# A hybrid S5, RWKV-7 and PEER decoder step on one core: dense pools opened with the last step, the sample's finish through a GpSimd transfer, finishing loads spread out, low-rank products of 64 rows, a last pick that is not held

## The chip, the cores and the metric

The kernel runs on one core of one Trainium2 chip. The metric is the device time of one execution in microseconds. It is written in Bass with the Tile framework.

## The reference, cut to what matters

One layer is run on a prompt (512 tokens) and on a sample group (8 x 8 = 64 tokens), d = 1024, float32. An adaLN-modulated RMSNorm feeds one input projection; its columns go to an S5 state-space mixer and to an RWKV-7 mixer of 8 heads. The low-rank part of RWKV that the change touches, and the PEER layer that takes most of the time:

```
w_raw = -softplus(-(w0 + tanh(w_lo) @ w2)) - 0.5      # w_lo: 64 columns
a = sigmoid(a0 + a_lo @ a2)                           # a_lo: 64 columns
...
q = (xb @ w_q).reshape(128, 8, 2, 64)                 # 8 retrieval heads
s1, s2 = q[:, :, 0] . keys1, q[:, :, 1] . keys2       # 128 keys each
v1, i1 = top_k(s1, 16); v2, i2 = top_k(s2, 16)
sc, pos = top_k(v1 + v2 over 16 x 16 pairs, 16)       # 16 of 16384 experts
idx = take(i1 * 128 + i2, pos); gate = softmax(sc)
act = gelu(einsum(u_tab[idx], xb))
ff = einsum(gate * act, v_tab[idx])
```

Then y = final RMSNorm(x + ga2 * ff), where x already holds the mixers' output.

## The kernel before, in words

Tokens are cut in tiles: tile 0 is the sample (64 tokens, held twice, so that each half of the partitions has four of the eight heads), tiles 1 to 4 are 128 prompt tokens each. They are taken in the order 1, 2, 3, 0, 4.

Phase 1 does the norm, the input projection and S5. Then five steps are woven: step i runs `back` (RWKV state) of a tile, `front` (RWKV's decay, keys and triangular inverse) of a later one, `select` (output projection, second norm, query and key scores), `pick` (the top 16s on VectorE) of the tile before, and `gbuild` of one of the tiles 1 to 3. `front` has the low-rank products (lines 923 to 928): W2 holds w2 in rows 0 to 63 of one half and a2 in rows 64 to 127 of the other, with zeros elsewhere; for each of the two halves four matmuls over 128 rows are followed by four activations.

Tiles 1, 2 and 3 (DENSE) go through all 16384 experts. `gbuild` writes their gates as a dense matrix: per 4 tokens (a step of its loop) two one-hot matrices B and A (tiles "ab") are made on ScalarE, VectorE or GpSimd, four matmuls multiply them, and ScalarE copies the result to Gst; per 16 tokens Gst goes to DRAM (Gd, line 1508). For the last of the three, the ab buffers are 15 in a pool of their own (gp2), and the 8 expert blocks of group 0 are copied from Gst into G0 (line 1505). `dense` then does 128 blocks of 128 experts: ur is 128 columns of u transposed; uh and ul are its rounded part and the rest; 24 matmuls give scores pd (line 1520); ScalarE applies gelu to wf (1605); VectorE multiplies the gates (1607); wf and the rows vr of v are split in the same way (1610 to 1623), and 18 matmuls add to the outputs po (1627), which stay in six PSUM banks. Blocks come in groups of 8 (GBL), each with its gates loaded from Gd (line 1525) at remainder 2 of the group before. The tokens' vectors hf are loaded, rounded and split to dh and dl once (1555, 1562, 1563).

Tiles 0 and 4 gather their experts' rows (`bulk`): 64 and 128 indirect loads of u rows on GpSimd's queue, a dot product on VectorE each (1449), gelu, then as many loads of v rows and accumulations (1459). Three gathers are issued per block. At the end of tile 0 two matmuls with a folding matrix add the two halves of acc (1465), ScalarE copies them to h2 (1466), and `finish` adds the residual, norms and stores. `finish` of the tiles 1 to 3 follows block 127. What `finish` needs is loaded by `open_finish`, one load per block from block 32 (FB).

The order of each engine's instructions is fixed when the program is built: Tile's scheduler models times and takes, per engine, what is ready in its model, the earlier line first. A pool that is opened takes memory that closed pools gave back, and its tiles wait for the tiles that were there. `issue_after(x)` keeps what is inside from being placed ahead of x. All loads and stores but the gathers and h2 are issued by SP.

Of the kernel before, what the change touches and what calls it, by code (L numbers as in the profile page):

```python
# [6 lines left out]
F32 = mybir.dt.float32  # L7
# [15 lines left out]
KB = 8  # L23
# [155 lines left out]
class Kernel:  # L179
# [6 lines left out]
    PB = {"r": 3, "s": 3, "h": 1, "g": 1}  # L186
    UX, UWT, AB2 = 0, 0.5, 15
    UG = True
    UO = -100000
    PO, GO, SO, RO, FO = {}, {}, {4: 4000}, {}, {}  # L190
    FB = 32
    PW = 3.0
# [10 lines left out]
    OHB = 2  # L203
    EU, ED = True, False
    UR = "s"
# [27 lines left out]
    def ps(self, shape, g="r"):  # L233
        t = (self.psA if g == "g" else self.psB).tile([128, 512], F32, name="pa" + g, bufs=self.PB[g])
        return shaped(t, shape[1:])[:shape[0]]
# [616 lines left out]
    def open_rwkv(self):  # L852
# [14 lines left out]
        SY.dma_start(rst, I["rst"])  # L867
        W2 = wp.tile([128, 2, 512], F32)
        g2 = wp.tile([128, 512], F32)
        G.memset(W2, 0.0)  # L870
        SY.dma_start(W2[0:64, 0, :], I["wa2"][0:64, :])
        SY.dma_start(W2[64:128, 1, :], I["wa2"][64:128, :])
        SY.dma_start(g2, I["g2"])
# [28 lines left out]
    def front(self, ti):  # L902
# [19 lines left out]
        sg = t4([8, W])  # L922
        for i in range(2):
            pz = ps([128, 4, W], "r")
            for j in range(4):
                T.matmul(pz[:, j, :], W2[:, i, j * 128:(j + 1) * 128], lt, start=True, stop=True)
            for j in range(4):
                S.activation(sg[:, 4 * i + j, :], pz[:, j, :], AF.Tanh, bias=hw0[:, 4 * i + j:4 * i + j + 1], scale=0.5)
# [504 lines left out]
    def bulk(self, ti, c0, nk, ei, gt):  # L1433
# [27 lines left out]
        if smp:  # L1461
            ffs = []
            for n in range(2):
                pf = self.ps([64, 512], "g")
                T.matmul(pf, self.fold, acc[:, n * 512:(n + 1) * 512], start=True, stop=True)
                S.copy(h2[:64, n * 512:(n + 1) * 512], pf)
            self.finish(0, [h2[:64]])
        else:
            self.finish(ti, [acc])

    def gbuild(self, d):
        V, S, G, T, SY = self.nc.vector, self.nc.scalar, self.nc.gpsimd, self.nc.tensor, self.nc.sync
        iob = self.iota[:, None, :].to_broadcast([128, 4, 128])
        n = self.TG
        gp, nb = (self.gp2, self.AB2) if d == 2 and self.AB2 else (self.gp, self.AB)
        for tg in range(128 // n):
            Gst = self.gs.tile([128, 128, n], F32, name="Gst")
            for q in range(n // 4):
                t0 = d * 128 + tg * n + q * 4

                def bc(t):
                    return t[:, t0:t0 + 4, None].to_broadcast([128, 4, 128])
                oh = gp.tile([128, 128, 4], BF16, name="oh", bufs=self.OHB)
                B = gp.tile([128, 4, 128], F32, name="ab", bufs=nb)
# [19 lines left out]
            if d == 2:  # L1504
                V.tensor_copy(self.G0[:, d * (128 // n) + tg], Gst[:, 0:self.GBL, :])
                if tg == 0:
                    self.loadG(self.G0, 0, d * (128 // n))
            SY.dma_start(self.Gd[d * (128 // n) + tg], Gst.rearrange("p n t -> p (n t)"))
# [19 lines left out]
    def open_dense(self):  # L1528
# [6 lines left out]
        if self.EU:  # L1535
            self.ue = sc.pool("ue", **kw)
        if self.ED:
            self.dp = sc.pool("dp", 1, **kw)
        self.G0 = sc.pool("g0", 1, **kw).tile([128, N // self.TG, self.GBL, self.TG], F32, name="G0")
        self.sh = Scope(self.tc)  # L1540
        self.hf = self.sh.pool("hf", **kw).tile([128, KB, N], F32, name="hf")
        if self.AB2:
# [10 lines left out]
        for d, ti in enumerate(self.DENSE):  # L1553
            sl = slice(128 * d, 128 * d + 128)
            SY.dma_start(self.hf[:, :, sl], self.h2d[ti].rearrange("p (k t) -> p k t", k=KB))

    def dense(self):
# [3 lines left out]
        N = 128 * nd  # L1561
        S.copy(self.dh, self.hf)
        V.tensor_tensor(self.dl, self.hf, self.dh.bitcast(F32), op=OP.subtract)
        self.sh.close()
# [3 lines left out]
        ue = self.ue if self.EU else sp.pool("ue", **kw)  # L1568
        up = sp.pool("up", 2, **kw)
        dp = self.dp if self.ED else sp.pool("dp", 1, **kw)  # L1570
        pso = sp.pool("pso", 1, space=PSUM, **kw)
# [7 lines left out]

        GO = dp.tile([128, N // TG, GBL, TG], F32, name="G1")  # L1580

# [12 lines left out]
        with self.tc.issue_after(self.kld.ins):  # L1594
            pa = first(0)
            G1 = self.G0
        for b in range(128):
            if b % GBL == 0:
                Gr = G1
            if b % GBL == self.GPF and b + GBL < 128:  # L1600
                with self.tc.issue_after(self.kld.ins):
                    G1 = (self.G0, GO)[(b // GBL + 1) % 2]
                    self.loadG(G1, b // GBL + 1)
# [26 lines left out]
        warm = self.sm.tile([128, 1], F32, name="ss")  # L1630
        S.activation(warm, self.iota[:, :1], AF.Sqrt)
        for d in range(nd):
            self.finish(self.DENSE[d], outs[2 * d:2 * d + 2], G if d in self.FP else V)

    def run(self, stop=None):
# [50 lines left out]
        else:  # L1686
            dense, gs = self.dense(), self.gathers()
            n = m = 0.0
            for b, r in enumerate(dense):
                m += self.PW  # L1690
                while m >= 1 and pk:
                    m -= 1
                    with tc.issue_after(self.gv.ins):
                        live = next(pk, 0)
                    if live == 0:
                        pk = None
                        self.sx.close()
                if b >= self.FB:
                    if b == self.FB:
                        fl = self.open_finish()  # L1700
                    with tc.issue_after(self.vld.ins):
                        next(fl, None)
# [40 lines left out]
```

## Time and profile before

| | us |
|---|---|
| median of 3 runs | 1920.74 (1916.82 to 1923.91) |
| the profiled execution: time / span | 1923.54 / 1921.8 |
| TensorE busy | 1771.2 (92%) |
| VectorE busy | 1512.5 (79%) |
| ScalarE busy | 803.6 (42%) |
| GpSimd busy | 676.7 (35%) |

The span is that of the profiled execution alone. A view by stretch gives the busy microseconds of each engine in it, TensorE's granted clock (1.00 is full speed), the busy share of the DMA engines and what they moved. In a timeline a bracket at the end of a row gives the idle time of the engine before it, and what ended it.

### The profile page before, as it was taken

How to read it: one execution, taken by the hardware profiler on the slowest of the kernel's cores; microseconds unless marked ns; L12 is line 12 of the kernel's file. 1: busy time of each engine (PE TensorE's matmuls, PEld its weight loads, DVE VectorE, ACT ScalarE, POOL GpSimd, SP SyncE). 2: the span in 40 equal slices, each digit the busy share in tenths (PEclk: the TensorE clock that was granted, in tenths of full speed). 3: DMA queues.
4: the chain of work that ended last, by engine and by line, in shares of the span. 5: the costliest groups of instructions: out<-in, count | busy, mean ns of one | idle time of the engine just before them, and what ended most of it. 6: DMA issues, size and time to landing. Idle time of an engine off the chain costs nothing.

```text
span 1921.8 us, 32723 instructions
## 1 busy us (share of the span) xinstructions
PE 1771.2 (92%) x12299; PEld 1531.6 (80%) x12299; DVE 1512.5 (79%) x3081; ACT 803.6 (42%) x1468; POOL 676.7 (35%) x540
## 2 busy tenths in 40 slices
PE   8899987988879797789999999999999999999994
PEld 5699645758558676779999998899999999999993
DVE  7958324495996968779988878798788878888898
ACT  4232515535764677733333333433333333333332
POOL 0000201000351334334544444364444445444554
PEclk9899998999889898989999999999999999999998
DMA  8524654544346586679999998899999999999995
GB/s 328 158 88 105 201 179 146 185 149 152 119 137 211 181 295 232 233 264 338 330 375 334 351 357 325 270 389 349 340 353 322 338 352 330 336 341 355 325 322 190
DMA packets 202206, 513.30 MB, mean 267 GB/s; under 512 B 26232, under 2 KB 87800, under 8 KB 197952
## 3 DMA queue, kind: packets, MB, share of 16 engines
q1 hardware_dynamic: 146464, 308.82, 47.1%
q0 software_dynamic: 55584, 202.40, 28.9%
q8 instruction: 96, 1.57, 0.3%
q14 instruction: 62, 0.51, 0.1%
HBM read 470.36 MB, written 39.62 MB: 265 GB/s over the span
## 4 chain that ended last, share of the span: by engine, by line
PE 52%; DVE 11%; issue 5%; POOL 4%; ACT 3%; DMA 2%; POOLq 0%; SPq 0%; ACTq 0%; DVEq 0%
PE pd L1520 24%; PE po L1627 23%; POOL gr L1444 3%; PE pas L1268 2%; DVE oh L1486 1%; DVE ab L1493 1%; DMA ur<-u_t 1%; DVE t2s L1306 1%; DVE idxu L1308 1%; DVE idxu L1305 1%; ACT ab L1490 1%; PE par L1501 0%; ACT Gst L1502 0%; PE pag L1501 0%; PE par L997 0%
## 5 line engine op out<-in xcount | busy, mean ns | idle before, releaser
L1444 POOL DMA_INDIRECT gr<-v_tab,ei x192 | 259.5, 1352 | 276.0 <-DVE acc L1459 246.4
L1520 PE MATMUL pd<-dh,uh 128*128 128x384 f32 x1024 | 346.3, 338 | 10.6 <-ACT wf L1605 10.6
L1520 PE MATMUL pd<-dh,ul 128*128 128x384 f32 x1024 | 345.7, 338 | 0.0
L1444 POOL DMA_INDIRECT gr<-u_tab,ei x192 | 247.3, 1288 | 278.4 <-DVE scr L1449 230.2
L1520 PE MATMUL pd<-dl,uh 128*128 128x384 f32 x1024 | 345.1, 337 | 0.0
L1516 ACT CAST uh<-ur 128x1024 fp32r<-128x1024 f32 x128 | 134.5, 1051 | 271.5 <-PE pd L1520 264.4
L1459 DVE SCALAR_TENSOR_TENSOR acc<-gr,act,acc 128x1024 f32<-128x1024 f32 x190 | 244.1, 1285 | 2.9 <-DMA gr<-v_tab,ei 1.5
L1627 PE MATMUL po<-vl,wh 128*128 128x512 f32 x768 | 237.8, 391 | 1.8 <-DVE vl L1623 1.8
L1627 PE MATMUL po<-vh,wl 128*128 128x512 f32 x768 | 236.7, 390 | 0.0
L1449 DVE SCALAR_TENSOR_TENSOR scr<-gr,h 128x1024 bf16<-128x1024 f32 x192 | 234.2, 1220 | 2.2 <-DMA gr<-u_tab,ei 1.3
L1517 DVE TENSOR_TENSOR ul<-ur,uh 128x1024 fp32r<-128x1024 f32 x128 | 157.3, 1229 | 71.5 <-ACT uh L1516 71.3
L1520 PEld LDWEIGHTS pd<-dh,uh 128*128 128x128 f32 x1024 | 194.0, 189 | 18.3 <-ACT wf L1605 12.4
L1627 PE MATMUL po<-vh,wh 128*128 128x512 f32 x768 | 200.3, 395 | 5.8 <-ACT vh L1622 5.8
L1520 PEld LDWEIGHTS pd<-dl,uh 128*128 128x128 f32 x1024 | 193.9, 189 | 4.9
L1610 ACT CAST wh<-wf 128x384 fp32r<-128x384 f32 x128 | 65.8, 514 | 311.8 <-PE po L1627 253.1
L1520 PEld LDWEIGHTS pd<-dh,ul 128*128 128x128 f32 x1024 | 193.7, 189 | 0.4
L1623 DVE TENSOR_TENSOR vl<-vr,vh 128x1024 fp32r<-128x1024 f32 x128 | 156.5, 1223 | 25.0 <-ACT vh L1622 24.8
L1627 PEld LDWEIGHTS po<-vl,wh 128*128 128x128 f32 x768 | 143.9, 188 | 33.8 <-DVE vl L1623 2.7
L1627 PEld LDWEIGHTS po<-vh,wl 128*128 128x128 f32 x768 | 144.2, 188 | 31.0
L1627 PEld LDWEIGHTS po<-vh,wh 128*128 128x128 f32 x768 | 141.2, 188 | 32.4 <-ACT vh L1622 9.3
L1622 ACT CAST vh<-vr 128x1024 fp32r<-128x1024 f32 x128 | 134.4, 1050 | 50.7 <-PE po L1627 38.2
L1498 POOL TENSOR_TENSOR ab<-oh,dix 128x512 f32<-128x512 bf16 x72 | 87.5, 1222 | 178.4 <-DVE oh L1486 64.2
(472 smaller groups left out, 2986.4 us busy)
## 6 DMA issues: line engine op xcount, KB each, us to landing
ur<-u_t SPq DMA_DIRECT2D x128, 512.0 KB
vr<-v_tab SPq DMA_DIRECT2D x128, 512.0 KB
Gd<-Gst SPq DMA_DIRECT2D x24, 1024.0 KB
G<-Gd SPq DMA_DIRECT2D x15, 1536.0 KB
wo<-w_out SPq DMA_DIRECT2D x40, 512.0 KB
wq<-w_q SPq DMA_DIRECT2D x40, 512.0 KB
wt<-w_ada SPq DMA_DIRECT2D x32, 512.0 KB
wr<-w_in SPq DMA_DIRECT2D x18, 512.0 KB
```

The lines of the kernel that those rows point to most:

```text
L1268: T.matmul(pt[:, hh, :], wq[:, k, :], hT[:, k, :], start=(k == 0), stop=(k == KB - 1))
L1444: G.indirect_dma_start(out=r, out_offset=None, in_=I[tab], in_offset=bass.IndirectOffsetOnAxis(ap=ei[:, k:k + 1], axis=0))
L1449: V.scalar_tensor_tensor(scr, r, 1.0, h2, op0=OP.mult, op1=OP.mult, accum_out=act[:, k:k + 1])
L1459: V.scalar_tensor_tensor(acc, r, act[:, k:k + 1], acc, op0=OP.mult, op1=OP.add)
L1498: G.tensor_tensor(A, oh, bc(self.dix[:, 1]), op=OP.mult)
L1516: nc.scalar.copy(uh, ur)
L1517: self.mark = nc.vector.tensor_tensor(ul, ur, uh.bitcast(F32), op=OP.subtract).ins
L1520: nc.tensor.matmul(pa, u[:, k, :], h[:, k, :], start=(k == 0 and i == 0), stop=(k == KB - 1 and i == 2))
L1610: S.copy(wh, wf)
L1622: S.copy(vh, vr)
L1623: V.tensor_tensor(vl, vr, vh.bitcast(F32), op=OP.subtract)
L1627: T.matmul(outs[2 * d + n], w[:, d * 128:(d + 1) * 128], v[:, n * 512:(n + 1) * 512], start=(b == 0 and i == 0), stop=(b == 127 and i == 2))
```

## The change

Pools `up` and `dp` are opened with the dense pools, before step 4, and both gate tiles lie there; hf becomes three parts that pass through the `ur` buffers. `gbuild` of the last tile copies the blocks of groups 0 and 1, and loads both groups' other tokens; it takes 4 ab buffers from gp2 for every third step and otherwise those of gp. The pick of tile 4 is not held behind the last gate instruction of VectorE. The finishing loads come one per 8 blocks from block 14. The sample's halves are added by a transfer and VectorE. Sqrt's table is asked for by an activation that reads the last wf.

```diff
-    UX, UWT, AB2 = 0, 0.5, 15
+    UX, UWT, AB2 = 0, 0.5, 4
-    FB = 32
+    FB = 14
-    EU, ED = True, False
+    EU, ED = True, True
@@ open_rwkv
-        W2 = wp.tile([128, 2, 512], F32)
+        W2 = wp.tile([128, 512], F32)
-        G.memset(W2, 0.0)
-        SY.dma_start(W2[0:64, 0, :], I["wa2"][0:64, :])
-        SY.dma_start(W2[64:128, 1, :], I["wa2"][64:128, :])
+        SY.dma_start(W2, I["wa2"])
@@ front
-        for i in range(2):
-            pz = ps([128, 4, W], "r")
-            for j in range(4):
-                T.matmul(pz[:, j, :], W2[:, i, j * 128:(j + 1) * 128], lt, start=True, stop=True)
+        pzs = [ps([128, 4, W], "r") for _ in range(2)]
+        for j in range(4):
+            for i in range(2):
+                sl = slice(64 * i, 64 * i + 64)
+                T.matmul(pzs[i][:, j, :], W2[sl, j * 128:(j + 1) * 128], lt[sl], start=True, stop=True)
+        for i, pz in enumerate(pzs):
@@ bulk
-            ffs = []
-            for n in range(2):
-                pf = self.ps([64, 512], "g")
-                T.matmul(pf, self.fold, acc[:, n * 512:(n + 1) * 512], start=True, stop=True)
-                S.copy(h2[:64, n * 512:(n + 1) * 512], pf)
+            G.dma_start(h2[:64], acc[64:128])
+            yield
+            V.tensor_tensor(h2[:64], h2[:64], acc[:64], op=OP.add)
             self.finish(0, [h2[:64]])
@@ gbuild
-        gp, nb = (self.gp2, self.AB2) if d == 2 and self.AB2 else (self.gp, self.AB)
+                gp, nb = (self.gp2, self.AB2) if d == 2 and (tg * n // 4 + q) % 3 == 2 else (self.gp, self.AB)
-                oh = gp.tile([128, 128, 4], BF16, name="oh", bufs=self.OHB)
+                oh = self.gp.tile([128, 128, 4], BF16, name="oh", bufs=self.OHB)
-                V.tensor_copy(self.G0[:, d * (128 // n) + tg], Gst[:, 0:self.GBL, :])
-                if tg == 0:
-                    self.loadG(self.G0, 0, d * (128 // n))
+                for g, t in enumerate(self.G2_):
+                    V.tensor_copy(t[:, d * (128 // n) + tg], Gst[:, g * self.GBL:(g + 1) * self.GBL, :])
+                    if tg == 0:
+                        self.loadG(t, g, d * (128 // n))
@@ open_dense
-        if self.ED:
-            self.dp = sc.pool("dp", 1, **kw)
-        self.G0 = sc.pool("g0", 1, **kw).tile([128, N // self.TG, self.GBL, self.TG], F32, name="G0")
+        self.up, self.dp = sc.pool("up", 2, **kw), sc.pool("dp", 1, **kw)
+        self.G2_ = [self.dp.tile([128, N // self.TG, self.GBL, self.TG], F32, name="G%d" % i) for i in range(2)]
-        self.hf = self.sh.pool("hf", **kw).tile([128, KB, N], F32, name="hf")
-            SY.dma_start(self.hf[:, :, sl], self.h2d[ti].rearrange("p (k t) -> p k t", k=KB))
+            hf = self.ud.tile([128, KB, 128], F32, name="ur", bufs=2)
+            SY.dma_start(hf, self.h2d[ti].rearrange("p (k t) -> p k t", k=KB))
+            S.copy(self.dh[:, :, sl], hf)
+            V.tensor_tensor(self.dl[:, :, sl], hf, self.dh.bitcast(F32)[:, :, sl], op=OP.subtract)
@@ dense
-        S.copy(self.dh, self.hf)
-        V.tensor_tensor(self.dl, self.hf, self.dh.bitcast(F32), op=OP.subtract)
-        up = sp.pool("up", 2, **kw)
-        dp = self.dp if self.ED else sp.pool("dp", 1, **kw)
+        up, dp = self.up, self.dp
-        GO = dp.tile([128, N // TG, GBL, TG], F32, name="G1")
-            G1 = self.G0
+            G1 = self.G2_[0]
             if b % GBL == self.GPF and b + GBL < 128:
-                with self.tc.issue_after(self.kld.ins):
-                    G1 = (self.G0, GO)[(b // GBL + 1) % 2]
+                G1 = self.G2_[(b // GBL + 1) % 2]
+                if b > GBL:
                     self.loadG(G1, b // GBL + 1)
-        S.activation(warm, self.iota[:, :1], AF.Sqrt)
+        S.activation(warm, wf[:, :1], AF.Sqrt, scale=0.0)
@@ run
-                    with tc.issue_after(self.gv.ins):
-                        live = next(pk, 0)
+                    live = next(pk, 0)
-                if b >= self.FB:
+                if b >= self.FB and b % 8 == self.FB % 8:
```

## Rows read from the trace of the kernel before

**Rows 1.** Stretches: start:end and length; busy us (x instructions) per engine; clock; DMA.
```profile
850.00:1886.00 1036.00, 1031.70 (x5197) 934.37 (x5197) 875.22 (x1092) 369.05 (x505) 495.56 (x375) 1.00 0.94 337
...
775.00:806.00 31.00, 24.67 (x206) 22.91 (x205) 26.04 (x93) 30.05 (x78) 15.58 (x12) 1.00 0.46 185
806.00:850.00 44.00, 33.53 (x146) 30.32 (x145) 36.04 (x173) 16.14 (x20) 10.44 (x10) 0.84 0.83 280
```

**Rows 2.** The chain of waits from 1800 us on: shares by line; start, us, what.
```profile
by line: issue 40.0%; POOL gr L1444 32.5%; DMA gr<-v_tab,ei 5.8%; DVE fx L1427 4.1%; POOL fx L1423 2.7%; DVE ss L247 2.1%; DVE acc L1459 1.0%; ACT L243 1.0%; DVE fx L1423 0.9%; ACT ft L1425 0.9%; DVE ft L1422 0.9%; DVE rs_t L245 0.7%; DVE r
...
1892.53 1.86 POOL gr L1444
```

**Rows 3.** The chain of waits, one steady dense block.
```profile
930.80 4.18 PE pd L1520 x24
934.99 4.12 PE po L1627 x18
```

**Rows 4.** Timeline of PE, first score matmul of blocks 0, 1, 3, 4.
```profile
805.89 0.42 PE L1520 MATMUL pd<-dh,uh 128*128 128x384 f32 x1
...
814.49 0.69 PE L1520 MATMUL pd<-dh,uh 128*128 128x384 f32 x1 [4.17 <-ACT wf L1605]
...
836.21 0.69 PE L1520 MATMUL pd<-dh,uh 128*128 128x384 f32 x1 [4.77 <-ACT wf L1605]
...
848.83 0.44 PE L1520 MATMUL pd<-dh,uh 128*128 128x384 f32 x1 [1.10 <-ACT wf L1605]
```

**Rows 5.** Timeline of ACT in the opening: casts that waited for loads.
```profile
810.64 1.05 ACT L1622 CAST vh<-vr 128x1024 fp32r<-128x1024 f32 x1 [2.93 <-DMA vr<-v_tab]
...
834.72 1.04 ACT L1516 CAST uh<-ur 128x1024 fp32r<-128x1024 f32 x1 [4.99 <-DMA ur<-u_t]
```

**Rows 6.** Timeline of SP's queue: gate stores before the first vr; a gate load.
```profile
781.77 22.23 SPq L1508 DMA_DIRECT2D Gd<-Gst  x5
804.05 1.39 SPq L1619 DMA_DIRECT2D vr<-v_tab  x2
...
815.46 0.38 SPq L1525 DMA_DIRECT2D G<-Gd  x1
```

**Rows 7.** Timeline of PE, 1100 to 1240: gaps; first of two fold matmuls.
```profile
1110.29 0.44 PE L1520 MATMUL pd<-dh,uh 128*128 128x384 f32 x1 [0.58 <-ACT wf L1605]
...
1166.07 1.65 PE L1627 MATMUL po<-vh,wh 128*128 128x512 f32 x6 [1.51 <-ACT vh L1622]
...
1211.91 1.07 PE L1465 MATMUL pag<-acc,con 128*64 128x512 f32 x2
...
1224.30 1.67 PE L1627 MATMUL po<-vh,wh 128*128 128x512 f32 x6 [1.61 <-ACT vh L1622]
```

**Rows 8.** The copies of line 1505: ns min/median/max, first and last start.
```profile
L1505 DVE COPY G<-Gst x8: 204/216/1068, 759.8 to 810.8; 128x128 f32<-128x128 f32 x8
```

**Rows 9.** Waits from 745 to 850: us in total, times, longest.
```profile
POOL ab L1498 <- PE par L1501: 12.2, 3, 7.0
```

**Rows 10.** The h2 loads of line 1440, issue to landing.
```profile
DMA to landing us min/median/max: 3.8/6.3/8.8
```

**Rows 11.** Timeline of ACT: loads of Sqrt's table at the sample's and the last finish.
```profile
1224.27 1.28 ACT L1631 ACT_TABLE_LOAD   x1
...
1903.53 1.28 ACT L243 ACT_TABLE_LOAD   x1
```

**Rows 12.** Timeline of DVE: the last accumulation.
```profile
1901.23 2.18 DVE L1459 SCALAR_TENSOR_TENSOR acc<-gr,act,acc 128x1024 f32<-128x1024 f32 x1
```

**Rows 13.** Timeline of PE: alternating halves of 64 rows; a front's low-rank products.
```profile
205.03 1.97 PE L767 MATMUL pas<-CL,Hs 64*72 64x128 f32 x32
...
208.99 2.00 PE L926 MATMUL par<-lt,W 128*128 128x128 f32 x16
```

**Rows 14.** Groups of DVE, 796 to 868, of tile 4's pick: busy us, mean ns.
```profile
L1308 DVE FIND_INDEX8 idxu<-vals,t2s 128x8 uint32<-128x128 f32 x16 | 4.3, 284 | 0.0
...
L1306 DVE MATCH_VALUE_LOAD t2s<-vals,t2s 128x8 f32 x16 | 1.2, 76 | 0.0
```

## The prediction

> **What bounds the kernel now.** I read the engine totals first, to see which engines could be the limit: TensorE and VectorE stand far above the others. An average over stages says little, so the stretches come next [rows 1]. From 850 to 1886 us (dense stage in its stride) TensorE is busy 1031.7 of 1036 us at granted clock 1.00, beside VectorE at 84% and DMA at 94%: TensorE bounds it, with little room on the other two. From 775 to 806 us (the end of the last gate build) TensorE has gaps and ScalarE is busy 30.05 of 31 us: ScalarE bounds it. From 806 to 850 us nothing is full, and the mean clock is 0.84: a stage of waits. So I looked there for what ends each wait of TensorE (its timeline), and then in the last 100 us with the chain of waits, which there runs through the GpSimd gathers and not through TensorE [rows 2].
>
> One dense block is 24 score matmuls in 4.18 us and 18 output matmuls in 4.12 us [rows 3], 8.30 us together. From the first score matmul at 805.89 to that of block 4 at 848.83 TensorE has 4 score and 3 output groups to do: 4 x 4.18 + 3 x 4.12 = 29.1 us. It takes 42.9. So 13.8 us are lost in the opening: gaps of 4.17, 4.77 and 1.10 us, all put down to the gelu's tile wf [rows 4], and some 3.8 us more in matmuls at the lower clock and a short gap. Behind the first gap ScalarE waited 2.93 us for block 0's rows vr, behind the second 4.99 us for ur [rows 5]. The reason for vr is on SP's queue: its issue comes after five gate stores that together hold the queue for 22.23 us [rows 6]. In mid-stage TensorE loses 0.58 and 1.51 us while the finishing loads run, and 1.61 us just after the sample's finish, whose two fold matmuls cost it 2 x 1.07 us [rows 7].
>
> **The change part by part.** The sum is against the profiled run's 1923.5 us (span 1921.8 and 1.7 around it), which is 2.8 us above the median of the three runs, 1920.7.
>
> *Pools from step 4 on.* Tiles up and dp no longer wait for hf and gp2, so block 0's vr, its cast vh, and block 1's uh and ul can be placed before 806, and group 1 of the gates is kept from the last build, so that the load of group 1 (24 x 8 x 16 x 128 values, 1536 KB) issued at 815.46 [rows 6] goes: 1536 KB at the 337 GB/s of the stage [rows 1] is 4.7 us of DMA in just the stretch where ur is late. The 13.8 us bound this gain; below it is nothing, if SP's order stays. The two long gaps, 8.9 us, end in the two loads that are brought forward or relieved. I take 9.
>
> What it adds in front of the opening: a second gate load of 1024 KB beside the first, 3.1 us of DMA at the same rate, where DMA is busy 46% [rows 1], so hidden unless it delays the w_q loads of the last select; three casts of about 1.05 us (one of them [rows 5]) moved onto a ScalarE with 1 us free in 31: up to 3.2 us; eight more copies from Gst, 0.216 us at the median and 1.068 at worst [rows 8], 1.7 to 8.5 us on a VectorE with 5 us free in that stretch. The last build's ab buffers go from 15 to 9 + 4; with 15, GpSimd already waits 12.2 us in three pieces for TensorE to free one [rows 9], so fewer cost 0 to 7.0, the longest of these once more. The hf copy in three parts is the same work as now, far from the end of its stage; but the third part waits for a ur buffer, and SP holds what is behind it: 0 to about 5 us, by the wait for ur [rows 5]. Most of these would fall into one another; I take +3, about the casts, since ScalarE is the full engine there, of 0 to 12. Net for the opening: -6.
>
> *Freer last pick.* The pick of tile 4 no longer stays behind the last gate instruction of VectorE. It may fill VectorE's 5 idle us [rows 1]: 0 at best for the end, and a price in the second rival. I take 0.
>
> *Spread finishing loads.* Eight steps, one every 8 blocks from block 14, instead of eight in a row from 32. The three that the sample's finish needs (x1, its gate, the final norm's row) come at blocks 14, 22 and 30; the fold runs at 1212 [rows 7], (1212 - 849) / 8.3 + 4, in block 48, so they are early. The same bytes in the same stage, away from the gate loads at block remainder 2: the 2.1 us (0.58 + 1.51) go. Bounds 0 and 2.1; I take -2.1.
>
> *Sample finish.* The fold's 2.1 us leave TensorE. In their place GpSimd issues a transfer of 64 rows from acc to h2, and VectorE adds. Behind that transfer on GpSimd wait the h2 load of tile 4 and its later gathers; behind the add on VectorE wait the splits ul, wf, wl and vl of the dense blocks, and TensorE behind them. The nearest row is GpSimd's own h2 load: 3.8 to 8.8 us to landing [rows 10]. Today that place costs VectorE a wait too (the finish's first product waits for the copies of the fold's halves), and TensorE 1.61 us after it; the new wait begins sooner, since nothing queues on TensorE between. Bounds: -3.7 (fold and stall both gone) to +3 (8.8 us of landing, less about 4 us that TensorE has in the score group of the next block [rows 3], less what is lost now). Sqrt's table load that was placed here for the end (at 1224.27, 1.28 us [rows 11]) moves behind the last gelu and with it a reload of gelu. I take -3.1.
> The Trainium skill, "SBUF — State Buffer", section "SBUF: two separate sides", warns that a DMA issued from GpSimd can be held while VectorE keeps a shared port, and gives some 620 ns alone against 3100 ns beside a VectorE copy, which speaks against this edit. The trace agrees in part at most: with VectorE 84% busy, a gather's issue lasts 1.86 us at the most seen in the chain [rows 2]. By the page's figure, an estimate, the transfer lands 2.5 us later and the whole sum is -9.7 instead of -12.2; by the rows it is inside the landing times above.
>
> *Sqrt's table at the end.* It is loaded once more today in the last finish, 1.28 us between the sum of squares and the root [rows 11]. Loaded before, it leaves that chain, but VectorE has a product to do beside it, and the last acc, at 1901.23 [rows 12], comes just before it. Bounds: -4 (two accumulations like the last one earlier, 2.18 us each beside GpSimd's adds, if the gathers profit from an earlier start) and +2 (they lag by one more). I take -1.
>
> *Low-rank products.* Eight matmuls of a front, 16 passes, take 2.00 us over 128 rows; where matmuls of 64 rows alternate between halves, 32 passes take 1.97 us [rows 13]. So about 1 us of TensorE goes in each of 5 fronts. But ScalarE's first activation still begins about 1 us after the first matmul, because both halves now end together, and it then has the same eight to do. Bounds: -5 (all five on the path) to +3 (a second "r" bank held). I take 0. One memset and one transfer at the start have nothing waiting for them: 0.
>
> Sum: -6 - 2.1 - 3.1 - 1 = -12.2, so 1911.3 on the profiled run's footing and, 2.8 lower, 1908.5 as a median.
>
> **The rivals.** *The opening stays.* The pools are free but the loads don't come sooner, since on SP's queue the gate stores stand ahead of vr [rows 6], and ur is late because the gathers' 512 KB pieces want the DMA as well. For it: the 22.23 us on SP; against it: the loads may be placed before those stores, and 1536 KB less are moved. Then the opening gives 0, and the rest -6.2: 1914.5.
>
> *VectorE takes the last pick first (the slower side).* If scores of tile 4 are ready while the last gates are built, VectorE works on the pick between them. Its first part is five groups of 16 selections, 4.3 us for the costliest, three of them with value loads of 1.2 us [rows 14]: at most 25 us; less the 5 us of idle time the gates are 20 us later, and by the eight copies at their worst 8.5 more. Against that stand the 9 of the opening, 5.2 of mid-stage and 1 at the end: +13.3, 1934. From some 7 us of the pick beyond that idle time (with the copies at worst) nothing is gained. For it: nothing but order holds the pick back today, and VectorE is busy 26 of 31 us there [rows 1]. Against: it comes after the gates in the program's order, and ScalarE, not VectorE, is full there.
>
> *Everything opens.* All 13.8 us go with no price in front, mid-stage gives its 5.8 (fold, loads, stall), the gathers start sooner since they wait today for ul of block 1, the end gives 4, the fronts 3: -26.6, so 1894.
>
> **How the numbers follow.** Forecast 0.52, opening stays 0.24, pick first 0.13, everything opens 0.11. About 0.5% (9.6 us) is what a measurement tells from no change: below 1911.1 is faster, above 1930.3 slower. Faster: 0.47 of the forecast, 0.02 of the second case, all of the last: 0.60. Slower: 0.09, of the pick's case. Same: 0.31. The forecast's own range is 1901 to 1915. Eight in ten needs the opening that stays, half of the pick's case and half of the full gain: 1896 to 1922.
>
> **What would show it.** The distance from the first score matmul of block 0 to that of block 4: 34 us or so instead of 42.9, with ScalarE's waits for vr and ur gone and no gate load among blocks 0 to 7. The first score matmul no later than 809. No fold matmuls; TensorE's gaps between the opening and block 126 under 2 us in all instead of 4.3 (1036 - 1031.7). At the handover a VectorE wait for the new transfer, below 5 us. No table load in the last finish. Wrong it would be if score matmuls begin after 815, if VectorE shows selections of the pick ahead of gate products, or if a wait on the transfer stops TensorE by more than 3 us.

## The result, and the profile after

The changed kernel takes 1901.01 us (median of 4 runs, 1899.56 to 1903.32); the kernel before took 1921.72 beside it. The ratio is 0.9891, 95% interval [0.9869, 0.9914]: about 20.7 us faster. The profiled spans are 1901.5 and 1921.8 us. The forecast, 1908.5, had the sign right and lies 7.5 us too high.

Between fixed points of the two timelines the 20.3 us of the spans divide so: the last load of the keys, which starts the last step's scores, at 764.40 instead of 768.61 (-4.2); from there to the first score matmul of block 16, 173.5 instead of 178.6 (-5.1); block 16 to block 120, 868.0 instead of 873.2 (-5.2); block 120 to the last output matmul, 72.2 instead of 79.2 (-7.0); from there to the end, 23.4 instead of 22.2 (+1.2). At both blocks the kernel before has one output group fewer done (14 against 15 at block 16, 118 against 119 at block 120): 4.12 us of TensorE's work that it does in the last stretch and not in the opening. Counted by work done, the opening gave -9.2 and the last blocks -2.9.

Stretches of the kernel after, columns as in [rows 1]:

```profile
838.00:1868.00 1030.00, 1028.60 (x5191) 933.76 (x5190) 863.92 (x1083) 369.82 (x500) 485.47 (x371) 1.00 0.94 339
773.00:804.00 31.00, 22.97 (x155) 21.14 (x154) 29.52 (x135) 23.10 (x54) 9.26 (x8) 0.84 0.59 231
804.00:838.00 34.00, 31.24 (x154) 28.73 (x153) 33.74 (x136) 14.15 (x18) 17.75 (x14) 0.94 0.78 293
```

The dense stage has 1.4 idle us where it had 4.3. In the last 31 us of the gate build VectorE is now the full engine (29.52), not ScalarE (23.10): the reverse of [rows 1]. The opening is a stage of waits no more: TensorE is busy 31.24 of 34 us. Its first score matmuls of blocks 0, 1 and 4, then two later gaps:

```profile
804.30 0.67 PE L1519 MATMUL pd<-dh,uh 128*128 128x384 f32 x1
...
813.17 0.45 PE L1519 MATMUL pd<-dh,uh 128*128 128x384 f32 x1 [2.76 <-ACT wf L1601]
...
838.20 0.33 PE L1519 MATMUL pd<-dh,uh 128*128 128x384 f32 x1
...
1226.60 0.73 PE L1623 MATMUL po<-vh,wh 128*128 128x512 f32 x2 [1.17 <-ACT vh L1618]
...
1873.63 0.50 PE L1623 MATMUL po<-vh,wh 128*128 128x512 f32 x1 [1.14 <-ACT vh L1618]
```

Block 0 to block 4 takes 33.9 us instead of 42.9, and one gap is left of the three of [rows 4]; of the gaps of [rows 7] one of 1.17 remains. On SP's queue vr now stands ahead of the gate stores, and the next gate load comes at 871.68 instead of 815.46 [rows 6].

```profile
764.40 0.33 SPq L1272 DMA_DIRECT2D keys<-keys  x1
764.78 0.90 SPq L1512 DMA_DIRECT2D ur<-u_t  x2
765.73 1.39 SPq L1615 DMA_DIRECT2D vr<-v_tab  x2
...
785.30 20.32 SPq L1507 DMA_DIRECT2D Gd<-Gst  x4
...
871.68 0.38 SPq L1524 DMA_DIRECT2D G<-Gd  x1
```

On ScalarE no cast waits for a load there any more [rows 5]; what holds wf now is the cast uh ahead of it in the queue, which waits for TensorE's score matmuls, and gelu's table load:

```profile
810.27 1.04 ACT L1515 CAST uh<-ur 128x1024 fp32r<-128x1024 f32 x1 [5.00 <-PE pd L1519]
811.33 1.28 ACT L1601 ACT_TABLE_LOAD   x1
812.63 0.49 ACT L1601 ACTIVATE wf<-pd 128x384 f32<-128x384 f32 x1
```

The granted clock differs too. Before, it fell to 0.50, the lower of its two levels (1.2 of 2.4 GHz), in each of the two long gaps, and the matmuls behind them ran at that level. After, it is 0.50 up to 808 us, behind gaps at the end of the gate build, and 1.00 in the rest of the opening. Two stretches of before, then two of after:

```profile
812.00:822.00 10.00, 7.51 (x27) 7.42 (x27) 8.29 (x36) 3.37 (x5) 4.84 (x5) 0.66 0.80 251
834.00:842.00 8.00, 5.79 (x20) 5.80 (x21) 6.21 (x23) 3.54 (x5) 1.14 (x2) 0.57 0.57 187
...
798.00:808.00 10.00, 8.77 (x34) 8.48 (x35) 10.00 (x69) 1.76 (x3) 1.30 (x2) 0.50 0.23 93
808.00:838.00 30.00, 27.24 (x140) 24.73 (x139) 29.74 (x107) 13.56 (x17) 17.75 (x14) 1.00 0.83 306
```

The sample's finish has no fold. GpSimd issues the transfer in 0.57 us, VectorE waits 0.27 us for it. GpSimd then stands idle for 11.92 us before the h2 load of tile 4, which waits until the finish has read h; before, that idle time was 12.27 us.

```profile
1173.80 1.22 DVE L1619 TENSOR_TENSOR vl<-vr,vh 128x1024 fp32r<-128x1024 f32 x1
1174.18 0.57 POOL L1462 DMA_DIRECT2D h<-acc  x1 [0.69 <-DVE acc L1459]
...
1182.32 1.22 DVE L1464 TENSOR_TENSOR h<-h,acc 64x1024 f32<-64x1024 f32 x1 [0.27 <-DMA h<-acc]
...
1187.96 0.57 POOL L1440 DMA_DIRECT2D h<-h2d  x1 [11.92 <-DVE ft L1422]
```

At the end Sqrt's table is loaded before the last finish [rows 11], and the last accumulation [rows 12] comes 18 us earlier, with GpSimd's three adds beside it:

```profile
1870.09 1.28 ACT L1627 ACT_TABLE_LOAD   x1
...
1877.41 9.87 POOL L1423 TENSOR_TENSOR fx<-fx,ft 128x1024 f32<-128x1024 f32 x3 [2.87 <-DVE ft L1422]
...
1883.20 1.89 DVE L1459 SCALAR_TENSOR_TENSOR acc<-gr,act,acc 128x1024 f32<-128x1024 f32 x1
```

A front's low-rank products take 1.16 us instead of 2.00 [rows 13]:

```profile
207.93 1.16 PE L925 MATMUL par<-lt,W 64*128 64x128 f32 x16
```

### The profile page after: what moved, and what is told of

Read it like the earlier page. It is cut to its first block, busy times and chain, and to the rows that moved or that the text cites. A ratio compares the mean times of both kernels' runs of the same rounds, so it can differ in the third digit from the quotient of the medians.

```text
span 1901.5 us, 32478 instructions
## 1 busy us (share of the span) xinstructions
PE 1765.9 (93%) x12295; PEld 1525.1 (80%) x12295; DVE 1507.7 (79%) x3092; ACT 802.6 (42%) x1466; POOL 674.6 (35%) x540
## 4 chain that ended last, share of the span: by engine, by line
PE 34%; issue 15%; DVE 12%; POOL 11%; ACT 3%; DMA 2%; POOLq 0%; SPq 0%; DVEq 0%; ACTq 0%
PE pd L1519 15%; PE po L1623 15%; POOL gr L1444 10%; PE pas L1268 2%; DVE oh L1484 1%; DVE ab L1491 1%; DMA gr<-v_tab,ei 1%; DMA vr<-v_tab 1%; DVE idxu L1305 1%; DVE t2s L1306 1%; DVE idxu L1308 1%; DVE vals L1304 1%; DVE vals L1307 1%; ACT ab L1488 0%; PE pah L1499 0%
## 5 line engine op out<-in xcount | busy, mean ns | idle before, releaser
L1444 POOL DMA_INDIRECT gr<-v_tab,ei x192 | 251.4, 1310 | 274.4 <-DVE acc L1459 245.8
L1444 POOL DMA_INDIRECT gr<-u_tab,ei x192 | 252.6, 1316 | 268.4 <-DVE scr L1449 240.9
L1623 PE MATMUL po<-vl,wh 128*128 128x512 f32 x768 | 233.2, 390 | 0.0
L1623 PE MATMUL po<-vh,wl 128*128 128x512 f32 x768 | 232.1, 390 | 0.0
```

The lines of the kernel that those rows point to most:

```text
L1444: G.indirect_dma_start(out=r, out_offset=None, in_=I[tab], in_offset=bass.IndirectOffsetOnAxis(ap=ei[:, k:k + 1], axis=0))
L1623: T.matmul(outs[2 * d + n], w[:, d * 128:(d + 1) * 128], v[:, n * 512:(n + 1) * 512], start=(b == 0 and i == 0), stop=(b == 127 and i == 2))
```

## The experiments

My first theory was that the stretches above add up: the pools bring the opening, the loads and the fold mid-stage. The rival was that the edits change the order which the scheduler writes, so that they don't add. All kernels are in this table. "Keys" is the time of the last keys load; the next two columns go from it to block 16's first score matmul and from there to the last output matmul; "lag" is how long after that the last accumulation of tile 4 ends; "tail" is from the last output matmul to the end. All but medians and ratios are of the profiled execution.

| kernel | median us | ratio to before, 95% | keys | to block 16 | to last output | lag | tail |
|---|---|---|---|---|---|---|---|
| before | 1921.7 | | 768.6 | 178.6 | 952.4 | 3.8 | 22.2 |
| after | 1901.0 | 0.9891 [0.9869, 0.9914] | 764.4 | 173.5 | 940.2 | 7.0 | 23.4 |
| pools_only | 1910.3 | 0.9937 [0.9913, 0.9960] | 765.9 | 166.9 | 950.5 | -2.0 | 21.0 |
| no_pools | 1915.6 | 0.9967 [0.9949, 0.9986] | 761.4 | 181.1 | 938.6 | 18.4 | 30.3 |
| pick_held | 1908.9 | 0.9916 [0.9892, 0.9941] | 766.4 | 162.0 | 959.5 | -7.7 | 21.1 |
| low_padded | 1917.2 | 0.9974 [0.9956, 0.9992] | 764.1 | 166.4 | 957.3 | -10.2 | 21.0 |
| held_inturn | 1897.8 | 0.9882 [0.9866, 0.9898] | 763.2 | 166.1 | 936.4 | 19.8 | 31.3 |
| after_inturn | 1905.6 | 0.9926 [0.9912, 0.9941] | 758.5 | 172.9 | 942.9 | 12.4 | 26.5 |
| sqrt_early | 1904.5 | 0.9911 [0.9895, 0.9926] | 766.1 | 174.0 | 940.9 | 7.1 | 23.5 |
| loads_in_row | 1902.4 | 0.9907 [0.9893, 0.9921] | 761.7 | 172.8 | 943.3 | 0.5 | 22.0 |
| before_inturn | 1918.8 | 0.9993 [0.9980, 1.0005] | 763.5 | 178.0 | 944.9 | 12.3 | 26.4 |
| held_padded_inturn | 1906.2 | 0.9923 [0.9906, 0.9940] | 766.5 | 168.2 | 938.1 | 16.0 | 29.3 |
| held_fold_inturn | 1901.1 | 0.9896 [0.9876, 0.9916] | 764.0 | 165.9 | 938.4 | 18.4 | 30.2 |
| held_inturn_rate | 1901.7 | 0.9903 [0.9886, 0.9920] | 757.8 | 165.6 | 936.0 | 12.8 | 35.9 |

The keys column needs care. The first keys load of the five kernels with zero rows in the low-rank product scatters from 365.0 to 371.1 us, that of the nine without from 370.7 to 377.6, and what follows moves along. So medians some 3 us apart tell little, while the stretches can be compared. One thing has to be minded there: at block 16 before, pools_only, pick_held and low_padded have 14 output groups done and the other ten kernels 15, so that these four show 4.1 us less in "to block 16" and 4.1 us more in "to last output" for the same work.

**The pools alone, and all but the pools.** Both ran on one chip.

```diff
# pools_only: before with these hunks (and those of GO, G0, hf) alone
+    UX, UWT, AB2 = 0, 0.5, 4
+        self.up, self.dp = sc.pool("up", 2, **kw), sc.pool("dp", 1, **kw)
# no_pools: before with all the other hunks
```

> The kernel before with the pools alone (up, dp, both gate groups, the copy in three parts, fewer buffers in the last gate build); the pick stays held, the fold, the loads in a row, the padded low-rank weights and the early root stay. Theory A (the terms of the two traces add): the first score matmul within 2 us of 805.9, the distance from block 0 to block 4 at 34 us instead of 42.9, mid-stage and end as before: 11.8 us off, so 1908 to 1911. Theory B (the price in front that I forecast is real, and the other edits pay it in the changed kernel): the first score matmul at 808 to 812 and so 1913 to 1917. The rival 'opening stays' of the prediction: distance still above 40 us, 1920 or more.

> All edits but the pools: pick free, loads spread from block 14, transfer instead of the fold, low-rank without zero rows, root's table at the end. Theory A: opening as before (42 to 43 us from block 0 to block 4), mid-stage loss down by 4 to 5 us, ends together between -2 and +2: 8 us off at the most, 1914 to 1918. Theory B (the other edits also bring the last select forward): first score matmul 3 to 8 us before 805.9, and so 1907 to 1913.

Measured: -10.7 and -5.4 us (of 1920.99). Together that is 16.1 where the change gave 20.7; the intervals are too wide to tell these apart. Both medians lie where theory A put them, but neither theory has the parts right. The pools bring block 16 forward by 11.7 us, 6.5 of them ahead of the first score matmul (30.8 us after the keys load instead of 37.3), where I had priced a loss. What in them does that was not taken apart; GpSimd's longest wait for TensorE to free an ab buffer in that stretch is 3.4 us in pools_only, 7.0 before. The other edits bring TensorE's last output 11.3 us nearer to the keys load (1119.7 instead of 1131.0, by the table) and get only 5.4 of it: the last accumulation comes 18.4 us behind TensorE. On GpSimd the last gathers stand behind its adds for the dense finishes:

```profile
1880.52 3.31 POOL L1423 TENSOR_TENSOR fx<-fx,ft 128x1024 f32<-128x1024 f32 x1
1883.98 1.74 POOL L1444 DMA_INDIRECT gr<-v_tab,ei  x1 [0.16 <-issue]
1885.74 2.35 POOL L1423 TENSOR_TENSOR fx<-fx,ft 128x1024 f32<-128x1024 f32 x1
1888.25 1.75 POOL L1444 DMA_INDIRECT gr<-v_tab,ei  x1 [0.16 <-issue]
1890.31 1.54 POOL L1444 DMA_INDIRECT gr<-v_tab,ei  x1 [0.30 <-issue]
```

So there are two chains to the end: TensorE's blocks, and the gathers of tile 4. The table shows it over all kernels but one: the tail is 21.0 to 21.1 where the accumulations end first, and grows with the lag (3.8: 22.2; 7.0: 23.4; 12.4: 26.5; 16.0: 29.3; 19.8: 31.3). From its first gather to its last accumulation, the gather chain takes 1086.4 us before, 1091.4 in no_pools, 1073.4 in pools_only and 1073.8 after: the pools shorten it by 13, and it is the opening that they speed up (32 gathers issued by 900 us in pools_only, 25 before). Counted from the keys load, the last accumulation ends 19.3 us sooner in pools_only than before, and 17.4 sooner after than in no_pools. Of the two halves, only the pools bring both chains forward.

The distance from block 0 to block 4 alone does not show what the pools do. In no_pools it is 35.7 us, although vr still comes behind the gate stores and ScalarE still waits for ur; there the first score matmul comes 45.6 us behind the keys load, so that the loads have 8.3 us more to land than before. From the keys load to block 4 it is 80.2 us before, 81.4 in no_pools, 67.2 in pools_only and 73.8 after, with 42, 54, 48 and 54 output matmuls done.

```profile
771.30 30.63 SPq L1506 DMA_DIRECT2D Gd<-Gst  x5
801.99 4.22 SPq L1617 DMA_DIRECT2D vr<-v_tab  x2
...
830.94 1.05 ACT L1514 CAST uh<-ur 128x1024 fp32r<-128x1024 f32 x1 [4.48 <-DMA ur<-u_t]
```

**The pick held again.** One line back in the changed kernel.

```diff
-                    live = next(pk, 0)
+                    with tc.issue_after(self.gv.ins):
+                        live = next(pk, 0)
```

> The changed kernel with the last pick held behind the last gate instruction of VectorE again. If the pick's selections between the gate products cost the last gate build what its select had gained (keys loaded 4 us earlier in the last step, 12.8 in the step before, first score matmul only 1.6 earlier): first score matmul at 798 to 802, and 1897 to 1900. If the selections sit in VectorE's idle time: within 1 us of the changed kernel's 1901.0. If the held pick delays the h2 transfer and the gathers behind it at the end: 1902 to 1905.

Measured: 1908.94, a miss. Block 16 does come 11.5 us sooner than in the changed kernel, and then TensorE takes 19.3 us longer to its last output; 4.1 of both is the output group that it does later. Between 1024 and 1080 us it is busy 51.74 of 56 us; with the groups in turn (below) it is busy throughout:

```profile
1024.00:1080.00 56.00, 51.74 (x253) 44.92 (x252) 46.66 (x46) 16.95 (x25) 35.41 (x22) 1.00 0.92 334
```

```profile
1024.00:1080.00 56.00, 56.00 (x284) 50.80 (x283) 45.39 (x47) 19.84 (x28) 24.91 (x20) 1.00 0.96 348
```

The timeline of the first kernel there shows blocks of 9.4 us instead of 8.30:

```profile
1032.06 0.52 ACT L1606 CAST wh<-wf 128x384 fp32r<-128x384 f32 x1 [6.46 <-PE po L1623]
...
1032.52 1.04 ACT L1618 CAST vh<-vr 128x1024 fp32r<-128x1024 f32 x1
...
1033.61 1.67 PE L1623 MATMUL po<-vh,wh 128*128 128x512 f32 x6 [0.79 <-ACT vh L1618]
```

TensorE's order is 12 output matmuls, 2 score matmuls, 6 output matmuls, 22 score matmuls: ScalarE's cast wh waits for the 12, vh stands behind wh, and TensorE has only two score matmuls to do meanwhile. That order is in the program: six such blocks in a row at one place, five at another.

**Zero rows in the low-rank product again.**

```diff
-        W2 = wp.tile([128, 512], F32)
+        W2 = wp.tile([128, 2, 512], F32)
+        G.memset(W2, 0.0)
-                T.matmul(pzs[i][:, j, :], W2[sl, ...], lt[sl], start=True, stop=True)
+                T.matmul(pz[:, j, :], W2[:, i, ...], lt, start=True, stop=True)
```

> The changed kernel with the zero rows back in the low-rank product (2.00 instead of 1.16 us of TensorE a front). My prediction's value (hidden, 0): 1900.5 to 1901.5. If the 0.84 us in each of 5 fronts lie on the path: 1905. If it is this edit that brought the keys loads of steps 2 to 4 forward by 27, 12.8 and 4.2 us: the keys loads go back to those of the kernel before and the time to 1903 to 1908.

Measured: 1917.24. The profiled execution took 1910.5, so that some 7 us of the median are not in it. In it the loss is again the split groups: 957.3 us instead of 940.2, 4.1 of them the output group that is done later, and 10.0 us more from the keys load to the last output. The keys loads of steps 3 and 4 go back from 572.7 and 673.3 to 595.3 and 676.8 us, the last one does not (764.1). The theory that the terms add has fallen: an edit in the fronts costs 13 us in the dense stage by the order that comes of it. So the next runs fix that order.

**TensorE's groups in turn.** `self.pdl` is the last score matmul issued, `self.pol` the last output matmul.

```diff
-                with self.tc.issue_after(self.kld.ins):
+                with self.tc.issue_after(self.kld.ins), self.tc.issue_after(self.pol.ins if b else self.kld.ins):
                     pa = first(b + 1)
+            with self.tc.issue_after(self.pdl.ins):
                 ... the 18 output matmuls
```

> The changed kernel with the pick held again and TensorE's groups put in turn by hand: the 18 output matmuls of a block in one piece behind the 24 score matmuls of the next block, those of the block after behind them. Theory A (the pick's selections cost 6 to 7 us before the first score matmul, and the held kernel gave that back because its order split the output groups for 6 blocks at two places, 14 us in all): first score matmul at 797 to 799, no row of gaps of 0.79 us behind vh, PE's end at 1872 to 1877, and 1893 to 1898 in all. Theory B (the gaps come from late rows of v or late VectorE, and only show where the order lets them): the same loss elsewhere, 1906 to 1911.

> The changed kernel, pick free, with TensorE's groups put in turn by hand as in held_inturn. Theory A: the changed kernel's own order loses only 4.6 us in all behind the opening, so nothing is to be had: first score matmul at 803 to 806, 1899 to 1903. Theory B (the groups must be free to change places where VectorE or a gate load is late): gaps of TensorE behind vl and wl of 5 us or more, 1906 or later.

Measured: 1897.78 (1896.40 to 1900.67) and 1905.61 (1902.54 to 1910.97), on one chip. With the pick held, block 16 keeps its gain, no row of 0.79 us gaps is left, and the stretch behind it falls from 959.5 to 936.4: theory A. TensorE's last output comes 19.0 us nearer to the keys load than in pick_held, and the median falls by 11.2, since the gathers now end last (lag 19.8). With the pick free, theory A fails: besides the later opening there is one gap of 4.75 us, behind the sample's finish. VectorE waits there for a gather of tile 4; behind that wait stands the gate product wf, for which the cast wh waits, and vh stands behind wh:

```profile
1210.17 1.22 DVE L1449 SCALAR_TENSOR_TENSOR scr<-gr,h 128x1024 bf16<-128x1024 f32 x1 [7.99 <-DMA gr<-u_tab,ei]
...
1214.56 0.79 PE L1624 MATMUL po<-vh,wh 128*128 128x512 f32 x1 [4.75 <-ACT vh L1618]
```

Side by side, the two say what the freer pick costs while TensorE's groups are in turn: 7.8 us, with that gap included. In the scheduler's own order the kernel with the free pick has the lower median, 1901.0 against 1908.9, and the intervals overlap. From the keys load to the first score matmul, held and then free:

```profile
763.20:795.90 32.70, 29.18 (x233) 27.77 (x232) 24.26 (x79) 31.40 (x77) 13.13 (x11) 0.95 0.82 307
```

```profile
758.50:797.60 39.10, 31.06 (x233) 29.20 (x231) 32.88 (x138) 31.56 (x77) 12.42 (x11) 0.91 0.68 259
```

VectorE has 8.6 us more to do, and it is the pick: its selections sum to 19.1 us in the second stretch and to 8.8 in the first. In the changed kernel itself GpSimd waits for the one-hots oh behind it, 17.9 us between those two points against 8.0 in held_inturn:

```profile
POOL ab L1496 <- DVE oh L1484: 17.9, 6, 4.9
```

**Sqrt early again.** TensorE's order stays that of the changed kernel.

```diff
-        S.activation(warm, wf[:, :1], AF.Sqrt, scale=0.0)
+        S.activation(warm, self.iota[:, :1], AF.Sqrt)
```

> The changed kernel with the root's table asked for early again, as in the kernel before; TensorE's order is the same. The prediction's step: one table load of 1.28 us comes back in the chain of the last finish and one in mid-stage, +1, bounds -2 to +4: 1902. If the load is hidden behind VectorE's last accumulations and products, which set the end in the changed kernel: 1901 within 0.5.

Measured: 1904.53 (1898.76 to 1906.31). The load is back in the last finish, and the tail is the same, 23.5 against 23.4: while it runs, VectorE has products and accumulations of the last finishes to do. The other 3 us of the median are inside the scatter of the first keys load (377.6 here, 376.4 in the changed kernel's profile). The step is worth nothing that shows.

```profile
1884.91 1.28 ACT L243 ACT_TABLE_LOAD   x1
```

**Loads in a row again.**

```diff
-    FB = 14
+    FB = 32
-                if b >= self.FB and b % 8 == self.FB % 8:
+                if b >= self.FB:
```

> The changed kernel with the finishing loads in a row from block 32 again; order as in the changed kernel up to about block 25. The prediction's step: TensorE's gaps of 0.58 and 1.51 us come back, +2.1: 1903. If the loads only matter through the order that the planner writes around them: no gap that ends in a late load, but groups split again (gaps of 0.79 behind vh), 1906 to 1915.

Measured: 1902.41, near the forecast for the step (its interval overlaps the changed kernel's), but by the other mechanism. Blocks 16 to 120 take 871.2 instead of 868.0 us, with a run of TensorE's gaps of 0.08 us and one of 0.79, all behind vh, while the loads run; no gap of 1.5 us there. In the kernel before, too, the gap of 1.51 us ends in a cast vh that stood directly behind a gelu and waited for no load:

```profile
1164.60 0.49 ACT L1605 ACTIVATE wf<-pd 128x384 f32<-128x384 f32 x1 [4.13 <-PE pd L1520]
1164.98 1.04 ACT L1622 CAST vh<-vr 128x1024 fp32r<-128x1024 f32 x1
```

The lag falls to 0.5, so the tail gives 1.4 back. The gap of 0.79 us:

```profile
1175.98 0.51 PE L1623 MATMUL po<-vh,wh 128*128 128x512 f32 x1 [0.79 <-ACT vh L1618]
```

**The kernel before with its groups in turn.** The edit is that of held_inturn, made in the kernel before.

> The kernel before with TensorE's groups put in turn by hand and nothing else. If order alone gives what mid-stage and the last blocks gave the changed kernel: loss behind block 4 down from 12.3 to 4 us or less, PE's end 7 to 9 us nearer to the last keys load; but the gathers of tile 4 then set the end as in no_pools (last accumulation 1131 to 1136 us after the last keys load), so 1916 to 1920. If the finishing loads and the fold are what TensorE waits for: gaps of 2 us at the loads and 1.6 us behind the fold stay, 1919 to 1922.

Measured: 1918.82, 0.9993 [0.9980, 1.0005]. TensorE's last output comes 8.0 us nearer to the keys load, although a gap of 2.67 us stays (again a cast vh, in ScalarE's order behind a gelu that waits for scores); the lag grows from 3.8 to 12.3, the tail from 22.2 to 26.4. Order alone buys no time that can be measured, because the gathers have not moved: their last accumulation ends 1135.3 us after the keys load, 1134.8 before.

**Zero rows and fold on the held kernel in turn.** The edits are those of low_padded and, for the fold:

```diff
-            G.dma_start(h2[:64], acc[64:128])
-            yield
-            V.tensor_tensor(h2[:64], h2[:64], acc[:64], op=OP.add)
+            for n in range(2):
+                pf = self.ps([64, 512], "g")
+                T.matmul(pf, self.fold, acc[:, n * 512:(n + 1) * 512], start=True, stop=True)
+                S.copy(h2[:64, n * 512:(n + 1) * 512], pf)
```

> held_inturn with the zero rows back in the low-rank product. If the low-rank edit is worth nothing by itself (the prediction's 0) and low_padded was slow by its order alone: last keys load within 3 us of held_inturn's 763.2 and 1896 to 1900. If it is worth the 16 us that low_padded lost, or a good part: 1904 or more.

> held_inturn with the fold's two matmuls and ScalarE's copies back at the sample's finish. The prediction's step: 2.1 us of fold and 1.6 us of stall come back on TensorE, 1900 to 1902 if TensorE sets the end. If the gathers of tile 4 set the end of held_inturn (its last accumulation stands 19.8 us behind PE's end): TensorE ends 2 to 4 us later, the time stays within 1 us of held_inturn's 1897.8.

Measured: 1906.21 and 1901.13. With the fold, its two matmuls are back and block 16 to the last output takes 2.0 us more; there is no stall behind them. The time's interval overlaps that of held_inturn, so what the fold costs the kernel is not settled; on TensorE it is 2.0.

```profile
1182.18 1.07 PE L1464 MATMUL pag<-acc,con 128*64 128x512 f32 x2
...
1188.30 1.07 PE L1464 MATMUL pag<-acc,con 128*64 128x512 f32 x2
```

The zero rows cost 5.1 us against the fold's kernel on the same chip (1903.4 to 1908.8 against 1896.0 to 1904.9), more than I gave them: keys 2.5 us later, block 16 another 2.3. The two kernels differ in the fold as well; against held_inturn, by the ratios to before, it is some 8 us, and there the intervals don't overlap. Over all 14 profiles the last keys load comes at 765.7 on average with zero rows and at 762.6 without: 10.1 us less from the first keys load to the last (388.3 instead of 398.4, each within 2.1), 7.0 more ahead of the first. Why the time ahead of the first grows wasn't tried.

**More gathers a block.** The aim was the lag of held_inturn.

```diff
-    RATE = 3.0
+    RATE = 3.1
```

> held_inturn with 3.1 gathers a block instead of 3, so that the last four no longer stand behind GpSimd's adds of the last finishes. If the gathers set the end of held_inturn: last accumulation before or at PE's end, the end 21 us behind PE's end, 1889 to 1893. If VectorE or the DMA can't take more in mid-stage (VectorE 84%, DMA 94% busy): gaps of TensorE behind wl, vl or vh of 5 us or more, 1896 or later.

Measured: 1901.65. The last four gathers no longer stand behind adds, the last accumulation ends 7.9 us sooner after the keys load (1114.4 instead of 1122.3), TensorE has no new gap, and the end doesn't come sooner: a tail of 35.9 us. VectorE now takes tile 4's finish first, and the dense finishes, whose outputs lay ready at 1859.4, start behind it:

```profile
1869.57 2.61 DVE L1459 SCALAR_TENSOR_TENSOR acc<-gr,act,acc 128x1024 f32<-128x1024 f32 x2 [1.19 <-DMA gr<-v_tab,ei]
1872.20 1.22 DVE L1422 TENSOR_TENSOR ft<-acc,fg 128x1024 f32<-128x1024 f32 x1
1873.35 1.28 DVE L1422 TENSOR_TENSOR ft<-po,fg 128x512 f32<-128x512 f32 x2
```

It is the exception to the tail's rule: VectorE's order of the finishes sets this end. Of the versions tried held_inturn is the fastest, 1897.8; its interval overlaps the changed kernel's, so that it beats that one is not shown.

## Why the prediction was right, and where its terms were off

**The opening, forecast -6 as -9 and +3.** From the keys load to block 16 the change gave -5.1, near the sum, by other parts, and -9.2 if the output group that before still owed there is counted. The loads came forward as said (vr ahead of the gate stores, the gate load of group 1 gone), and the distance of blocks 0 to 4 is the 34 us named. But I counted three output groups done in it before; only 42 of 54 output matmuls were, so 2.75 us of TensorE's work were still owed and the gain was larger. The distance is no proof of the loads alone, since no_pools has 35.7. The price in front, +3, I gave to ScalarE's casts. The first score matmul does come 2.6 us later after the keys load (39.9 instead of 37.3), but for another reason: the pools alone bring it 6.5 us nearer, and the freer pick took that back (32.7 held and 39.1 free, with the groups in turn).

**The freer pick, forecast 0.** Mis-sized: it costs 7.8 us with TensorE's groups in turn. The prediction had the mechanism as its slower rival, with VectorE busy on selections ahead of the gates and a price beyond its 5 idle us; I let "ScalarE is full there" speak against it, a fact of the kernel before that the same edit changes. The sign that I named for being wrong, selections of the pick ahead of gate products, is in the trace.

**Finishing loads -2.1 and sample finish -3.1.** Blocks 16 to 120 gave -5.2, just their sum, and the wait for the transfer was 0.27 us where I allowed 5. Singly the loads are 3.2 us of that stretch and the fold 2.0 with the groups in turn, one above its forecast and one below, so the agreement of the sum is partly chance. The loads' mechanism was wrong: I read the gaps of 0.58 and 1.51 us as loads in the way, but the gelu and the cast in which they end had waited for scores and not for a load. From the transfer's issue to VectorE's add it took 8.1 us (1174.18 to 1182.32), inside the landing times of [rows 10]. The longest issue of a gather in the dense stage before was 2.14 us, not the 1.86 that I took from its end. The Trainium skill's page "SBUF — State Buffer", section "SBUF: two separate sides", gives some 3100 ns for a DMA issued from GpSimd that overlaps a VectorE copy. The one transfer here was issued in 0.57 us while VectorE ran the split vl of 1.22 us, so this trace shows no hold; the split is no copy, so the page's own case was not run. One gather behind it did take 4.45 us to issue (at 1197.10); why was not tried.

**Low-rank products, forecast 0.** Mis-sized: about 3 us at the last keys load over the 14 profiles, 5.1 in the median of the one pair with the groups in turn, which differs in the fold as well. I looked at ScalarE's first activation only, and the order of steps 2 to 4 moved.

**Sqrt's table, forecast -1.** The load left the chain, and the tail did not shorten: worth nothing that shows.

**What the sum did not have.** The last blocks: -7.0 from block 120 on. Before, the score groups ran a block further ahead there, so that three output groups were left for the end, with three gaps (1.13, 1.27 and 1.13 us); after, there is one of 1.14. One of the three groups, 4.1 of the 7.0 us, is work that the opening had left over; 2.9 are a gain of this place. And the end itself: I read from [rows 2] that the chain runs through the gathers, then summed TensorE's gains as if they were the time. The experiments show that TensorE's gain alone is worth little (8.0 us of it gave no time in before_inturn, 11.3 gave 5.4 in no_pools); it became time because the pools, by starting the gathers' steady pace sooner, shortened the other chain by 13 us. That the time lies in the range that I gave, at its lower edge (1901 of 1901 to 1915), is in part luck: the order in which the scheduler wrote the groups is no term of my sum, and with one edit taken back it gave 1908.9 (pick_held) and 1917.2 (low_padded).

Of the rivals, "the opening stays" is out, "VectorE takes the last pick first" was half true, and "everything opens" named the gathers' earlier start, which is what let the change pay.

## What to carry to other kernels

Where two chains end within a few microseconds of each other, price an edit on both, and expect the one that moves a single chain to pay only up to the other. Where a scheduler writes each engine's order, an edit anywhere can reorder a stage that it doesn't touch; look at the order of groups there, and fix it by hand, before one term is compared with another. An engine's idle time in the trace of before is not free for what an edit adds: here 10 us of selections went into 5 us of it, ahead of the work that others waited for.

## What the runs showed that I had not expected

Seven of the kernels differ from the changed one in order only from the last gate build on, and yet the first keys load of these eight comes anywhere from 370.7 to 377.6 us, while the distance from that load to the last one stays within 386.3 and 390.4: of the scatter up to the last keys load, more is made in the first 375 us than in the next 390. Why was not tried. And a transfer on GpSimd's queue was issued in 0.57 us while VectorE ran a split.
